# Softmax factors of a forgetting-attention layer: the 12-element steps move from GpSimd to VectorE

## The chip, the cores and the metric

The kernel runs on one core of one Trainium2 chip. The metric is the device time of one execution in microseconds (us). TensorE is called PE below (its weight loads PEld), VectorE DVE, ScalarE ACT, GpSimd POOL and the queue of transfers SP.

## The reference

One decoder layer over 1040 tokens (16 learned ones in front of 1024 real ones), width 1024, all in float32. A normalised input is projected to q, k, v, a forget gate, an output gate z and four inputs of a gated convolution. Attention has 8 heads of 64:

```
s = einsum('bqhd,bkhd->bhqk', q, k) * scale + c[t] - c[s]      # c: running sum of log forget gates
s = where(key_pos <= t, s, -inf)
p = softmax(s, axis=-1);  out = einsum('bhqk,bkhd->bqhd', p, v)
```

The attention output and the convolution output are RMS-normalised by groups of 64 columns, multiplied by SiLU gates, concatenated, sent through one output projection, added to the residual and normalised.

## The kernel before

Every float32 product is made of three matmuls over a high part and a low part of each operand. The program has three stretches. Up to some 178 us it projects q, k, v and the gate. From 178 to 480 us it sweeps the 8 heads. Then comes the output projection.

The middle stretch is what the change touches. For each head the queries are taken in two halves, `c = 0` (query blocks 0 to 3) and `c = 1` (blocks 4 to 7), so there are 16 half-heads. The half with `c = 1` of a head comes first. For one half:

- `s_step` (lines 605 to 614): for a block of 128 queries j and a chunk i of its keys (`SCH[j]`, one to three chunks), two matmuls make the scores in a PSUM bank `pn`, DVE takes their negated row maximum into `nmx[c]` (L609 for the last chunk, which is masked, L612 for the others), ACT writes exp(score - chunk maximum) into the SBUF tile `pn[j]` and the sum of each row into `smx[c]` (L613).
- `s_end` (lines 616 to 636) comes once per half, so 16 times. It turns the 4 x 3 chunk maxima and sums of a row into a factor per chunk: row maximum `mx` (L619, DVE), difference `e` (L621, POOL), its exp (L622, ACT), `e` times the sums `t` (L624, POOL), their sum over three chunks `s` (L626 and L627, two additions on POOL), reciprocal (L628, DVE), factor `fc` (L630, POOL). Then POOL multiplies each chunk of `pn[j]` by its factor (L635: 9 pieces for `c = 1`, 5 for `c = 0`).
- `t_step` (L645 to L657): PE transposes a 128-key column of `pn[j]` for the blocks of the half into a PSUM bank `pt` (two buffers); at the diagonal DVE clears and transposes a 32-column corner (L649, L651); ACT writes the high part `ph` (L654), DVE the low part `pl` (L115, the helper `lo_vec`).
- `v_step` (L669): two matmuls of `ph` and `pl` with v into the bank `po`; `fold` (L680, L681) brings the two halves of `po` together.

Between these steps PE is given projection work of the other branch as filler: `block_steps` (L165, tile `pj`), three matmuls at a time, with its followers on DVE and ACT (the gate's SiLU at L433 to L438, the convolution at L451 to L467, group norms at L404 to L417). The weights of the next block are split into `wmhi` (L112, POOL) and `wmlo` (L115, DVE). The first convolution product `cv` is POOL's (L460), the next two and the scaling are DVE's (L461 to L463).

The order of PE's matmuls in this stretch is written out: `weave` mixes steps by given durations, and `pinned` keeps that order. `s_end` stands at a given place in it (`S_AT`, `WAIT`). The other engines' instructions are ordered by the framework's planner, from its own estimate of when each one's inputs are ready; each engine then works through its queue in that order. SP issues the loads of the next head's q, k, v and of weights; `s_end` issues no transfer.

Of the kernel before, what the change touches and what calls it, by code (L numbers as in the profile page):

```python
# [12 lines left out]
ALU = mybir.AluOpType  # L13
AX = mybir.AxisListType
# [3 lines left out]
P = 128  # L18
# [17 lines left out]
def hybrid_kernel(ctx, tc, hT, h, w_q, w_vf, w_m, w_o, gn, bf, cw, ga, gc, gf, out):  # L36
    nc = tc.nc
# [531 lines left out]
    nmx, smx = [], []  # L569
# [46 lines left out]
    def s_end(c):  # L616

        mx = pnp.tile([P, 4], F32, name="mx")
        nc.vector.tensor_reduce(mx, nmx[c], AX.X, ALU.min)  # L619
        e = pnp.tile([P, 4, 3], F32, name="e")  # L620
        nc.gpsimd.tensor_tensor(e, mx.unsqueeze(2).broadcast_to([P, 4, 3]), nmx[c], ALU.subtract)  # L621
        nc.scalar.activation(e, e, AF.Exp)  # L622
        t = pnp.tile([P, 4, 3], F32, name="t")
        nc.gpsimd.tensor_mul(t, e, smx[c])  # L624
        s = pnp.tile([P, 4], F32, name="s")
        nc.gpsimd.tensor_add(s, t[:, :, 0], t[:, :, 1])  # L626
        nc.gpsimd.tensor_add(s, s, t[:, :, 2])  # L627
        nc.vector.reciprocal(s, s)  # L628
        fc = pnp.tile([P, 4, 3], F32, name="fc", bufs=2)
        nc.gpsimd.tensor_mul(fc, e, s.unsqueeze(2).broadcast_to([P, 4, 3]))  # L630
        for i in range(3):
            for j in range(4 * c, 4 * c + 4):
                if i < len(SCH[j]):
                    k0, w = SCH[j][i]
                    nc.gpsimd.tensor_scalar(pn[j][:, k0:k0 + w], pn[j][:, k0:k0 + w], fc[:, j % 4, i:i + 1], 1.0,  # L635
                                            ALU.mult, ALU.mult)
# [79 lines left out]
    for g in range(-1, 2 * HEADS):  # L716
        steps = []
        if g >= 0 and g % 2 == 0 and g // 2 + 1 < HEADS:
            steps.append((0.0, 0.0, lambda hd=g // 2 + 1: load_head(hd)))
        if g + 1 < 2 * HEADS:  # L720
            hd, c = (g + 1) // 2, g % 2
            todo = [(2 * SCH[j][i][1] / 2400.0, lambda hd=hd, j=j, i=i: s_step(hd, j, i))
                    for j in range(4 * c, 4 * c + 4) for i in range(len(SCH[j]))]
            lo, hi = S_AT[g % 2 if g >= 0 else 2]
            spread(steps, todo, lo, hi)
            steps.append((hi, WAIT[g % 2 if g >= 0 else 2], lambda c=c: s_end(c)))
        if g >= 0:
            hd, c = g // 2, 1 - g % 2
            box = {}
            tv = []  # L730
            nk = 4 * c + 5
            for kt in range(nk + V_LAG):
                if kt < nk:
                    w = 512 - max(0, (kt - 4 * c) * P - 32)
                    tv.append((w / 1200.0, lambda c=c, kt=kt, box=box: t_step(c, kt, box)))
                if kt >= V_LAG:
                    w = 512 - max(0, (kt - V_LAG - 4 * c) * P - 32)
                    tv.append((w / 1200.0, lambda hd=hd, c=c, kt=kt - V_LAG, box=box: v_step(hd, c, kt, box)))
            spread(steps, tv, T_AT[c], V_END)
            steps.append((0.99, 0.0, lambda hd=hd, c=c, box=box: fold(hd, c, box)))  # L740
            if g > 0 and (g - 1) % 4 >= 2:
                steps.append((0.05, SOON, lambda m=(g - 1) // 4, c=g % 2: finish_soon(m, c)))
        stages.append([(x, s) for _, x, s in sorted(steps, key=lambda t: t[0])])
# [164 lines left out]
```

## Time and profile before

| | |
|---|---|
| median of 3 runs | 595.57 us (594.65 to 597.58) |
| profiled execution, its own time | 596.83 us |
| its span, first to last instruction | 595.1 us |
| PE busy in the span | 578.0 us (97%) |
| DVE busy | 377.9 us (64%) |
| ACT busy | 285.4 us (48%) |
| POOL busy | 168.0 us (28%) |
| mean granted TensorE clock | 0.995 |

A busy PE is not a PE at its peak: matmuls are pipelined and their ends are modelled. What PE really loses is seen in the distances between the starts of its instructions. A row of the timeline gives start, duration, engine, line, operation, output and inputs with their sizes, and behind it the idle time before it with what ended it.

### The profile page before, as it was taken

The page shows a single profiled execution, that of the slowest core. Times are in us where ns is not written, and L with a number is a line of the kernel's source. Part 1 is how long each engine was busy: PE and PEld are TensorE (multiplying, and loading weights), DVE is VectorE, ACT ScalarE, POOL GpSimd, SP SyncE. Part 2 cuts the span into 40 slices and gives each one's busy share as a digit, 9 for nine tenths or more (in the row PEclk, how much of TensorE's full clock was granted, in tenths as well). Part 3 has the DMA queues.
Part 4 walks back from the last instruction along what each step waited for, and adds up shares of the span by engine and source line. Part 5 has one row for each costly group of instructions (what it writes and reads, how often), then busy time and mean ns, then how long its engine had stood idle before and what let it go on. Part 6 is the DMA issues. An engine that isn't in the chain of part 4 may idle for free.

```text
span 595.1 us, 9156 instructions
## 1 busy us (share of the span) xinstructions
PE 578.0 (97%) x3230; PEld 509.6 (86%) x3230; DVE 377.9 (64%) x834; ACT 285.4 (48%) x667; POOL 168.0 (28%) x290
## 2 busy tenths in 40 slices
PE   9999999999998999999999999999999999899995
PEld 6888999999997889988879997889998887688884
DVE  5415851133367686879776888868869777947432
ACT  5355431131044575556764655747636676705221
POOL 1002010121027244151243254430552416710000
PEclk9999999999999999999999999999999999899999
DMA  8764594249811605415126134251350227453201
GB/s 287 237 194 141 195 341 142 70 147 280 262 39 36 144 35 135 120 57 155 44 75 143 71 108 112 75 143 37 111 197 16 73 88 243 171 205 113 100 35 70
DMA packets 35221, 78.14 MB, mean 131 GB/s; under 512 B 4024, under 2 KB 13384, under 8 KB 35176
## 3 DMA queue, kind: packets, MB, share of 16 engines
q1 hardware_dynamic: 35032, 77.57, 41.6%
q8 instruction: 25, 0.41, 0.3%
q14 instruction: 20, 0.16, 0.1%
q10 hardware_dynamic: 144, 0.00, 0.0%
HBM read 55.92 MB, written 21.64 MB: 130 GB/s over the span
## 4 chain that ended last, share of the span: by engine, by line
PE 71%; DMA 10%; DVE 6%; POOL 4%; ACT 3%; issue 3%; SPq 2%; POOLq 0%; ACTq 0%; DVEq 0%
PE pj L165 30%; PE ps L324 8%; PE p L788 8%; PE pt L645 5%; PE po L669 5%; PE pj L788 4%; PE ps L165 4%; DMA k<-kd 3%; DMA ht<-in_h 3%; PE pn L605 3%; PE pn L606 3%; DMA xs<-in_hT 2%; DVE mlo L115 2%; POOL pn L635 1%; DMA wm<-in_w_m 1%
## 5 line engine op out<-in xcount | busy, mean ns | idle before, releaser
L165 PE MATMUL pj<-xhi,wmhi 128*128 128x512 f32 (+1 forms) x384 | 144.9, 377 | 1.0 <-DVE kf L275 0.5
L165 PE MATMUL pj<-xhi,wmlo 128*128 128x512 f32 (+1 forms) x384 | 137.1, 357 | 0.0
L165 PE MATMUL pj<-xlo,wmhi 128*128 128x512 f32 (+1 forms) x384 | 136.8, 356 | 0.0
L613 ACT ACTIVATE pn<-pn,nmx 128x328 f32<-128x328 f32 (+6 forms) x112 | 60.5, 541 | 52.7 <-DVE nmx L612 27.9
L165 PEld LDWEIGHTS pj<-xhi,wmlo 128*128 128x128 f32 x384 | 72.2, 188 | 8.4
L165 PEld LDWEIGHTS pj<-xhi,wmhi 128*128 128x128 f32 x384 | 72.6, 189 | 6.2 <-issue 1.4
L165 PEld LDWEIGHTS pj<-xlo,wmhi 128*128 128x128 f32 x384 | 72.8, 190 | 3.8
L654 ACT CAST ph<-pt 128x512 fp32r<-128x512 f32 (+4 forms) x112 | 49.6, 445 | 51.0 <-PE po L669 23.3
L635 POOL TENSOR_SCALAR pn<-pn,fc 128x328 f32<-128x328 f32 (+4 forms) x112 | 69.3, 639 | 1.6
L115 DVE TENSOR_TENSOR pl<-pt,ph 128x512 fp32r<-128x512 f32 (+1 forms) x96 | 54.6, 572 | 20.2 <-ACT ph L654 19.5
L112 POOL TENSOR_SCALAR wmhi<-wm 128x1024 fp32r<-128x1024 f32 x24 | 26.2, 1093 | 141.2 <-DMA wm<-in_w_m 81.8
L645 PE MATMUL pt<-ident,pn 128*128 128x128 f32 x288 | 47.4, 273 | 3.9 <-POOL pn L635 2.2
L645 PEld LDWEIGHTS pt<-ident,pn 128*128 128x128 f32 x288 | 36.3, 140 | 14.4 <-POOL pn L635 3.6
L115 DVE TENSOR_TENSOR wmlo<-wm,wmhi 128x1024 fp32r<-128x1024 f32 x24 | 29.4, 1223 | 18.0 <-POOL wmhi L112 17.9
L609 DVE CUSTOM_DVE_ANT_0 pn<-pn,maskn 128x328 f32<-128x328 f32 (+3 forms) x64 | 31.9, 500 | 11.0 <-PE pn L606 9.3
L669 PE MATMUL po<-ph,v 128*128 128x512 f32 (+4 forms) x112 | 37.0, 336 | 0.0
L605 PE MATMUL pn<-k,q 128*128 128x328 f32 (+6 forms) x112 | 36.6, 328 | 0.1
L606 PE MATMUL pn<-k,q 66*128 66x328 f32 (+6 forms) x112 | 36.1, 322 | 0.0
L669 PE MATMUL po<-pl,v 128*128 128x512 f32 (+1 forms) x96 | 33.2, 350 | 0.0
L788 PE MATMUL p<-whi,mlo 128*128 128x512 f32 (+1 forms) x77 | 30.2, 392 | 2.4 <-DVE mlo L115 2.4
L165 PE MATMUL ps<-xhi,wmhi 128*128 128x346 f32 (+1 forms) x96 | 31.0, 323 | 1.1 <-ACT qraw L240 1.1
L612 DVE TENSOR_REDUCE nmx<-pn 128x1 f32<-128x346 f32 (+4 forms) x48 | 24.8, 521 | 9.6 <-PE pn L606 9.6
(227 smaller groups left out, 1229.5 us busy)
## 6 DMA issues: line engine op xcount, KB each, us to landing
wm<-in_w_m SPq DMA_DIRECT2D x24, 512.0 KB, 3.8
k<-kd SPq DMA_DIRECT2D x24, 260.0 KB, 5.3
q<-qd SPq DMA_DIRECT2D x24, 256.0 KB, 5.9
vd<-vv SPq DMA_DIRECT2D x9, 512.0 KB, 2.9
v<-vd SPq DMA_DIRECT2D x8, 576.0 KB, 6.5
ht<-in_h SPq DMA_DIRECT2D x8, 512.0 KB, 5.6
yd<-gy SPq DMA_DIRECT2D x16, 256.0 KB, 2.8
q<-in_w_o SPq DMA_DIRECT2D x8, 512.0 KB, 4.5
```

What stands on the lines that cost most here:

```text
L115: nc.vector.tensor_tensor(lo, src, f(hi), ALU.subtract)
L165: ins = nc.tensor.matmul(ps[:, :w], wt[:, k, :], xt[:, t0:t0 + w], start=(k == 0 and n == 0), stop=(k == KT - 1 and n == 2))
L324: nc.tensor.matmul(ps[c][:P if n == P else 48, :260], x[k][:, ts_] if n == P else x[:, k, :], w[k][:, 260 * c:260 * c + 260], start=(k == ...
L605: pinned(nc.tensor.matmul(ps[:, :w], q1[:, qs], k1[:, ks], start=True, stop=False))
L606: pinned(nc.tensor.matmul(ps[:, :w], q2[:DH + 2, qs], k2[:DH + 2, ks], start=False, stop=True))
L609: nc.vector.tensor_tensor_reduce(ps[:, :w], ps[:, :w], maskn[:, MASKW - w:], op0=ALU.add, op1=ALU.min, scale=-1.0, scalar=-NEG, accum_out= ...
L613: nc.scalar.activation(pn[j][:, ks], ps[:, :w], AF.Exp, bias=nmx[c][at], scale=-1.0 if last else 1.0, accum_out=smx[c][at])
L635: nc.gpsimd.tensor_scalar(pn[j][:, k0:k0 + w], pn[j][:, k0:k0 + w], fc[:, j % 4, i:i + 1], 1.0, ALU.mult, ALU.mult)
L645: pinned(nc.tensor.transpose(pt[:, q0:q0 + P], pn[j][:, ks], ident))
L654: nc.scalar.copy(ph[:, at:], pt[:, at:])
L669: pinned(nc.tensor.matmul(po[:, at:], v2[:, vk, :], t[:, at:], start=(kt == 0 and i == 0), stop=(kt == 4 * c + 4 and i == len(parts) - 1)))
L788: ins = nc.tensor.matmul(held[n][:, :w], a[:, tt], b[:, cs], start=(e == ORDER[0] and i == 0), stop=(e == ORDER[-1] and i == 2))
```

## The change

In `s_end` the four instructions on `e`, `t` and `fc` are issued on VectorE, and the two additions over the three chunks become one `tensor_reduce` there. The exp stays on ScalarE, the scaling of `pn` (L635) on GpSimd.

```
         mx = pnp.tile([P, 4], F32, name="mx")
         nc.vector.tensor_reduce(mx, nmx[c], AX.X, ALU.min)
         e = pnp.tile([P, 4, 3], F32, name="e")
-        nc.gpsimd.tensor_tensor(e, mx.unsqueeze(2).broadcast_to([P, 4, 3]), nmx[c], ALU.subtract)
+        nc.vector.tensor_tensor(e, mx.unsqueeze(2).broadcast_to([P, 4, 3]), nmx[c], ALU.subtract)
         nc.scalar.activation(e, e, AF.Exp)
         t = pnp.tile([P, 4, 3], F32, name="t")
-        nc.gpsimd.tensor_mul(t, e, smx[c])
+        nc.vector.tensor_mul(t, e, smx[c])
         s = pnp.tile([P, 4], F32, name="s")
-        nc.gpsimd.tensor_add(s, t[:, :, 0], t[:, :, 1])
-        nc.gpsimd.tensor_add(s, s, t[:, :, 2])
+        nc.vector.tensor_reduce(s, t, AX.X, ALU.add)
         nc.vector.reciprocal(s, s)
         fc = pnp.tile([P, 4, 3], F32, name="fc", bufs=2)
-        nc.gpsimd.tensor_mul(fc, e, s.unsqueeze(2).broadcast_to([P, 4, 3]))
+        nc.vector.tensor_mul(fc, e, s.unsqueeze(2).broadcast_to([P, 4, 3]))
```

(Three of the instructions, on `e`, `t` and `fc`, have two inputs in SBUF; the reduce has one.)

## Rows read from the trace of the kernel before

**Rows 1.** The page's chain that ended last: shares of the span by engine.
```profile
PE 71%; DMA 10%; DVE 6%; POOL 4%; ACT 3%; issue 3%; SPq 2%; POOLq 0%; ACTq 0%; DVEq 0%
```

**Rows 2.** Busy us (and instructions) by engine in the stretch of the heads.
```profile
178.00:480.00 302.00, 297.82 (x1663) 261.77 (x1662) 233.66 (x570) 177.44 (x451) 119.62 (x218) 1.00 0.33 97
```

**Rows 3.** Waits of PE and PEld, 178:480: who <- whom, us, times, longest.
```profile
PEld pt L645 <- POOL pn L635: 3.6, 4, 1.7
...
PE pt L645 <- POOL pn L635: 2.2, 2, 1.5
```

**Rows 4.** Instructions by line: xcount, ns min/median/max, first and last start us.
```profile
L621 POOL TENSOR_TENSOR e<-mx,nmx x16: 206/209/1239, 178.9 to 473.3; 128x12 f32<-128x12 f32 x16
...
L622 ACT ACTIVATE e<-e x16: 202/215/223, 179.2 to 474.0; 128x12 f32<-128x12 f32 x16
```

**Rows 5.** Timeline of DVE, 129:132, a chain of dependent additions.
```profile
131.03 0.76 DVE L362 TENSOR_TENSOR acc<-acc,lf 128x8 f32<-128x8 f32 x4
```

**Rows 6.** Timeline of POOL, 176:184.5, the first set of small steps.
```profile
178.95 0.21 POOL L621 TENSOR_TENSOR e<-mx,nmx 128x12 f32<-128x12 f32 x1
179.48 0.89 POOL L624 TENSOR_TENSOR t<-e,smx 128x12 f32<-128x12 f32 x1 [0.32 <-ACT e L622]
...
182.25 1.10 POOL L630 TENSOR_TENSOR fc<-e,s 128x12 f32<-128x12 f32 x1 [0.29 <-DVE s L628]
183.45 1.11 POOL L635 TENSOR_SCALAR pn<-pn,fc 128x328 f32<-128x328 f32 x2
```

**Rows 7.** Timeline of PE, 183:186.5, behind the first set.
```profile
183.97 0.28 PE L606 MATMUL pn<-k,q 66*128 66x272 f32 x1
185.76 0.66 PE L645 MATMUL pt<-ident,pn 128*128 128x128 f32 x4 [1.51 <-POOL pn L635]
```

**Rows 8.** Timeline of DVE, 296:301, the seventh set.
```profile
298.55 1.27 DVE L115 TENSOR_TENSOR wmlo<-wm,wmhi 128x1024 fp32r<-128x1024 f32 x1
299.78 0.19 DVE L628 RECIPROCAL s<-s 128x4 f32<-128x4 f32 x1
```

**Rows 9.** Timeline of PE, 301:304.5, behind the seventh set.
```profile
302.32 0.40 PE L165 MATMUL pj<-xlo,wmhi 128*128 128x512 f32 x1
302.55 0.39 PE L165 MATMUL pj<-xhi,wmlo 128*128 128x512 f32 x1
303.64 0.66 PE L645 MATMUL pt<-ident,pn 128*128 128x128 f32 x4 [0.70 <-POOL pn L635]
```

**Rows 10.** Timeline of PE, 382:383.5, behind the eleventh set.
```profile
382.77 0.40 PE L165 MATMUL pj<-xhi,wmlo 128*128 128x512 f32 x1
383.26 0.44 PE L645 MATMUL pt<-ident,pn 128*128 128x128 f32 x2
```

**Rows 11.** Timeline of DVE, 355.5:361, the tenth set.
```profile
355.52 0.69 DVE L115 TENSOR_TENSOR pl<-pt,ph 128x512 fp32r<-128x512 f32 x1
...
356.26 1.28 DVE L461 SCALAR_TENSOR_TENSOR cv<-cx,cwt,cv 128x1024 f32<-128x1024 f32 x1
...
359.77 0.18 DVE L628 RECIPROCAL s<-s 128x4 f32<-128x4 f32 x1 [0.66 <-POOL s L627]
359.91 0.62 DVE L115 TENSOR_TENSOR pl<-pt,ph 128x416 fp32r<-128x416 f32 x1
```

**Rows 12.** Timeline of POOL, 356:361.5, the tenth set.
```profile
356.37 1.24 POOL L621 TENSOR_TENSOR e<-mx,nmx 128x12 f32<-128x12 f32 x1
```

**Rows 13.** Timeline of PE, 359:361, during the tenth set.
```profile
359.64 0.39 PE L165 MATMUL pj<-xhi,wmlo 128*128 128x512 f32 x1
360.67 0.30 PE L645 MATMUL pt<-ident,pn 128*128 128x128 f32 x1 [0.64 <-DVE pl L115]
```

**Rows 14.** Timeline of PE, 355:364, the transposes that reuse the bank of 355.52.
```profile
357.81 0.38 PE L645 MATMUL pt<-ident,pn 128*128 128x128 f32 x2
```

**Rows 15.** Timeline of DVE, 455:460, the fifteenth set.
```profile
456.11 0.59 DVE L115 TENSOR_TENSOR pl<-pt,ph 128x416 fp32r<-128x416 f32 x1 [0.34 <-ACT ph L654]
```

**Rows 16.** Timeline of PE, 454:457.5, the transposes that reuse that bank.
```profile
456.85 0.30 PE L645 MATMUL pt<-ident,pn 128*128 128x128 f32 x1
```

## The prediction

> **What bounds the kernel now.** I read the page's chain first. PE holds 71% of it, POOL 4%, DVE 6% [rows 1]: the small steps can only be worth what PE waits for them, not what they last. The busy times of the stretch from 178 to 480 us say the same: of 302 us PE is busy 297.82, DVE 233.66 (77%), POOL 119.62 (40%) [rows 2]. Next the waits of PE and its weight loads in this stretch, for everything that ends with the scaled scores `pn`: four waits of the weight loads, 3.6 us, and two of matmuls, 2.2 us [rows 3]. The matmul's wait is the same stall as the weight load's, seen a second time, so there are four stalls in sixteen calls of `s_end`. Twelve calls hand over early enough that PE never waits for POOL.
>
> What each stall costs is read from PE's starts. Three-matmul groups of 512 columns go at 302.55 - 302.32 = 0.23 us each [rows 9]. A start later than that is lost time:
> - first set: 185.76 - 183.97, less 0.12 for 272 columns: 1.67 us [rows 7];
> - seventh set: 303.64 - 302.55 - 0.23 = 0.86 us [rows 9];
> - eleventh set: 383.26 - 382.77 - 0.23 = 0.26 us [rows 10];
> - the fifteenth repeats the pattern at 461.9 us with about 0.2 us.
>
> Together 2.99 us. One more stall hangs on the small steps by a detour. At 360.67 PE stands 360.67 - 359.64 - 0.23 = 0.80 us, not for `pn` but for a PSUM bank that DVE's `pl` still reads [rows 13]; this `pl` started at 359.91, behind a reciprocal that had DVE idle for 0.66 us until POOL's sum came [rows 11]. With it all that the change can win on the way of the factors is 3.8 us, 0.64% of the time.
>
> **The change part by part.**
>
> Removed from POOL: five instructions in each of 16 sets, some 0.21 us each where nothing disturbs them (the median of the difference) and up to 1.24 us where something does [rows 4], so 16 x 5 x 0.21 = 17 us of an engine that is 40% busy [rows 2]. By itself this is worth nothing; what counts is the time to the factor. Also gone are the crossings between POOL and DVE around the reciprocal.
>
> Added to DVE: four instructions a set. The nearest row is a chain of dependent additions of 128x8 on DVE: four in 0.76 us, 0.19 us each with the gap between them [rows 5]. The new shapes have 12 elements, so I take 0.19 us, with 0.16 (no gap) and 0.25 as bounds. That is 16 x 4 x 0.19 = 12.2 us, and takes DVE in this stretch from 233.66 to 245.8 us, 81%.
>
> The new time to the factor, from the start of `e` to the first `pn` piece: `e` 0.19; the two crossings to ACT and back together 179.48 - 179.16 - 0.215 = 0.10 (between POOL and ACT [rows 4, 6]; I take the same for DVE); the exp 0.215 [rows 4]; `t`, the sum, the reciprocal and `fc` 4 x 0.19 = 0.76; to POOL 183.45 - 183.35 = 0.10 [rows 6]. That is 1.37 us if nothing stands between. In the first set this piece took 183.45 - 178.95 = 4.50 us [rows 6].
>
> What the four stalls give back:
> - Seventh set: the reciprocal stood on DVE behind the split of a weight block, 1.27 us from 298.55, and started at 299.78 [rows 8]. With all steps on DVE in one run this one long instruction can still stand in front of one of them, but the sum no longer crosses engines ahead of it. I count all 0.86 us. Bounds 0 and 0.86.
> - Eleventh and fifteenth: 0.26 + 0.2 = 0.46 us, all of it, since a quarter of a microsecond is less than the steps get shorter. Bounds 0 and 0.46.
> - First set: here the POOL steps were stretched to 0.89 and 1.10 us [rows 6] in the time in which DVE worked on the convolution. The same shows in the tenth set: `e` took 1.24 us instead of 0.21 and ended at 357.61, just behind DVE's L461 at 357.54 [rows 11, 12]. POOL waits while DVE works on such an operand pair. The convolution's three instructions (L461 and its two followers) are still to be done, and the `pn` pieces, which start earlier now, meet them in place of the small steps. I take half of 1.67, 0.83 us. Bounds 0 and 1.67.
> - Tenth set: the wait of 0.66 us on DVE goes, but 4 x 0.19 = 0.76 us of new instructions come in front of the same `pl`. I take 0. Bounds -0.3 (if two of the steps follow a wait for the exp) and +0.80.
>
> Sum: 0.86 + 0.46 + 0.83 = 2.15 us won.
>
> [...]
>
> What it costs: DVE works in order, so each set puts 0.76 us of new work, and a wait for the exp of up to 0.10 + 0.215 = 0.32 us, in front of whatever is queued there: the `pl` of the running transposes, the followers of the projection blocks, then the next scores' maxima. Who waits is PE, for the bank that `pl` frees two transposes later. The spare time differs: the `pl` of 355.52 ended at 356.21, and the transposes that reuse its bank started at 357.81, 1.60 us later [rows 11, 14]; the one of 456.11 ended at 456.70 with 0.15 us to spare [rows 15, 16]. A delay of 0.76 + 0.32 = 1.08 us is hidden under 1.6 and not under 0.15, where 0.93 us would be lost. Near the sixteen sets I find the small spare time in two, the sixth (0.4 us) and the fifteenth; elsewhere it is 1.5 us or more. In the fifteenth DVE was idle for 0.34 us just before [rows 15], which takes up `e`. I count 0.9 us for both together. Bounds 0 and 1.9.
>
> Sum: -2.15 + 0.9 = -1.25 us. The profiled execution took 596.83 us (span 595.1 and 1.7 around it), so 595.6 by its own time; it lies 1.26 us over the median of 595.57, and against that median the forecast is 594.3 us, -0.2%. A measurement of this kernel tells about 0.5%, or 3 us, from no change, so this is no change that can be seen.
>
> **The rivals.**
> - *All stalls go.* The new 1.37 us hold everywhere, the pieces of the first set don't meet the convolution, DVE's work is hidden: -3.8 us, 591.8. For it: in each of these places the factors come late by a wait that the change takes away [rows 3, 6, 8, 11]. Against: rows 11 and 12, and that it needs all five places at once, with no cost.
> - *DVE waits in line for ACT.* A step that needs the exp stands directly behind `e`, and ACT has other work in front of the exp. Place: DVE's queue, in each set; price: delay less spare time. With 0.76 + 0.32 and half a microsecond of other work on ACT (one cast of `ph` or one exp of scores) the delay is 1.6 us: it equals the usual spare time [rows 11, 14], and from there on it decides. At 2.1 us, one instruction more, each of fourteen sets loses 0.5 and the two tight ones 1.9: 14 x 0.5 + 2 x 1.9 = 10.8; where this holds for every other set, 5.4, less the 2.15 won: +3.3 us, 598.8. For it: DVE is at 77% and goes to 81%, and 0.66 us of such idling are in the trace already [rows 11]. Against: the planner puts ready work between; at 298.55 it put 1.27 us of it in front of the reciprocal [rows 8].
> - *The lock moves on.* By that mechanism (rows 11 and 12) the first set gives nothing and the others as above: -0.4 us, 595.1.
> - *The order changes elsewhere.* Only PE's order is written out; the planner lays the other queues anew. A weight split or a convolution step that lands in front of a `pl` costs up to its 1.27 us [rows 8] less the spare time. It can go either way; I let it widen the range by 2 us on both sides.
>
> **How the numbers follow.** Forecast with the moved lock, between -3 and +3 us: 0.56. All stalls go, or nearly all with a lucky new order, beyond -3 us: 0.20. DVE's waiting or an unlucky order, beyond +3 us: 0.24. The range reaches from 591.4, a little below the case in which every stall goes, to 599.4, a little above the slower rival.
>
> **What would show it.** In the trace after: `e` to `pn` under 2.2 us in most sets; the four waits of the weight loads for POOL's `pn` down from 3.6 us to under 1.5, the first set's the largest left; POOL's `pn` pieces of the first set with durations over 1 us beside L461 to L463; DVE some 246 us busy in the stretch; new waits of PE for `pl` of about 1 us in all. The forecast is wrong if PE's waits for DVE grow past 4 us, or if those for `pn` vanish and none comes in their place.

## The result: 1.2% slower, and the profile after

The changed kernel took 602.43 us (median of six runs, 599.34 to 604.63) against 595.11 us for the kernel before beside it (593.98 to 597.58): a ratio of 1.0117, 95% interval 1.0080 to 1.0155. The forecast was 594.3 us with a range up to 599.4, so it was wrong, and on the wrong side. The profiled execution took 604.03 us with a span of 602.3 us, that of before 596.83 and 595.1: the two traces differ by about the same 7.2 us as the medians. From the reciprocal on, line numbers are one lower in the changed kernel (the factor is L629, `pn` is scaled in L634, transposed from L644 and multiplied with v in L668).

Busy times by engine (PE, PEld, DVE, ACT, POOL), then granted clock, DMA share and GB/s, of the same stretch, which now lasts to 488 us [rows 2]:

```profile
178.00:488.00 310.00, 302.80 (x1667) 265.04 (x1666) 242.41 (x635) 178.73 (x453) 99.24 (x138) 0.99 0.33 94
```

DVE has 8.8 us more work (12.2 were forecast; some of the added time overlaps its neighbours, as at 180.60 us below, where a step of 0.16 us is followed after 0.12) and POOL is relieved. PE has more to wait for: 7.2 us are not busy where there were 4.2, and some of its busy time runs at a lower clock (0.99 granted over the stretch, 1.00 before). The waits of PE and its weight loads in that stretch (who <- whom, us, times, longest) [rows 3]:

```profile
PEld pt L644 <- POOL pn L634: 6.4, 5, 2.4
PEld po L668 <- DVE ph L115: 1.6, 2, 0.9
PEld po L668 <- DVE pl L115: 1.0, 1, 1.0
```

The waits for `pn` that were to shrink from 3.6 us to under 1.5 grew to 6.4, and 2.6 us for `ph` and `pl` stand beside them. The steps themselves are as short as forecast in the median; three of the 48 with two inputs took longer, 0.28 to 0.58 us (count, ns min/median/max, first and last start) [rows 4]:

```profile
L624 DVE TENSOR_TENSOR t<-e,smx x16: 157/164/583, 181.9 to 481.7; 128x12 f32<-128x12 f32 x16
L626 DVE TENSOR_REDUCE s<-t x16: 148/166/197, 183.2 to 481.9; 128x4 f32<-128x12 f32 x16
L629 DVE TENSOR_TENSOR fc<-e,s x16: 158/172/395, 184.1 to 482.6; 128x12 f32<-128x12 f32 x16
```

So the steps are short, but the chain is long. From the start of the maximum (L619) to the end of the factor the mean over sixteen sets is 3.33 us before and 3.86 us after. The first set shows why; DVE's timeline (start, us, instruction):

```profile
178.37 0.16 DVE L619 TENSOR_REDUCE mx<-nmx 128x4 f32<-128x12 f32 x1
...
179.40 1.28 DVE L461 SCALAR_TENSOR_TENSOR cv<-cx,cwt,cv 128x1024 f32<-128x1024 f32 x1 [0.86 <-POOL cv L460]
180.60 0.16 DVE L621 TENSOR_TENSOR e<-mx,nmx 128x12 f32<-128x12 f32 x1
180.72 1.28 DVE L462 SCALAR_TENSOR_TENSOR cv<-cx,cwt,cv 128x1024 f32<-128x1024 f32 x1
181.92 0.16 DVE L624 TENSOR_TENSOR t<-e,smx 128x12 f32<-128x12 f32 x1
182.04 1.23 DVE L463 TENSOR_TENSOR cv<-cv,rbc 128x1024 f32<-128x1024 f32 x1
183.18 0.16 DVE L626 TENSOR_REDUCE s<-t 128x4 f32<-128x12 f32 x1
183.26 0.68 DVE L472 TENSOR_TENSOR zc<-pj,rbc 128x512 f32<-128x512 f32 x1
183.85 0.17 DVE L627 RECIPROCAL s<-s 128x4 f32<-128x4 f32 x1
...
184.15 0.17 DVE L629 TENSOR_TENSOR fc<-e,s 128x12 f32<-128x12 f32 x1
```

In front of every step that follows the maximum other work stands in DVE's queue, most of it long. Before, POOL's queue held only the steps in thirteen of the sixteen sets (in the sixth, seventh and eighth a weight split of 1.05 us stood among them), and only the maximum and the reciprocal passed through DVE's [rows 6, 8]. A late factor is not yet lost time: the tenth set's takes longest, 7.12 us instead of 4.10, and PE does not wait for it. What PE makes of it in the first set [rows 7], from PE's timeline:

```profile
184.35 0.28 PE L606 MATMUL pn<-k,q 66*128 66x272 f32 x1
...
186.80 0.66 PE L644 MATMUL pt<-ident,pn 128*128 128x128 f32 x4 [2.16 <-POOL pn L634]
```

The stretch behind it, busy by engine, with the granted clock as the third column from the end:

```profile
188.00:191.00 3.00, 3.00 (x11) 2.41 (x10) 2.08 (x3) 1.00 (x2) 2.37 (x4) 0.50 0.00 0
```

The stall is 186.80 - 184.35 - 0.12 = 2.33 us instead of 1.67. Then the granted clock fell to 0.50 (before, behind the stall of 1.67 us, it was 1.00 from 188 to 191 us), and PE's 512-column matmuls started 189.95 - 189.52 = 0.43 us apart instead of 0.23 (PE's timeline):

```profile
189.52 0.63 PE L165 MATMUL pj<-xlo,wmhi 128*128 128x512 f32 x1
189.95 0.63 PE L165 MATMUL pj<-xhi,wmlo 128*128 128x512 f32 x1
```

PE executes the same 3230 matmuls in the same order in both kernels, so each one's start can be compared. Of 7.38 us in all: the start-up +0.4; the first set +2.2 (0.65 stall, 1.6 clock); 267 us, before the sixth set, -0.9; the sixth +1.4; the seventh +0.6; the ninth +0.5; the tenth -0.4; 450 us +0.3; the fifteenth +3.4, of which 1.4 is clock (0.50 from 468 to 471 us); the rest -0.1. The -0.9 at 267 us is there in e4, e6 and e11 below as well, of which two leave the steps on POOL, so it does not come from the steps. Nor does it come from another order: DVE and POOL have the same instructions in the same order there in both traces. In the trace of before DVE's `gsl`, with two inputs in SBUF, lasts through a `pn` piece (264.75 to 265.31 us) and a weight split of POOL (265.27 to 266.32); in the trace after it starts 0.09 us ahead of that piece, which now takes 1.03 us instead of 0.56, and ahead of the split at 268.48 (DVE's timeline, before and after):

```profile
264.74 2.15 DVE L115 TENSOR_TENSOR gsl<-gy,gsh 128x512 fp32r<-128x512 f32 x1 [1.16 <-ACT gsh L407]
```

```profile
267.39 0.69 DVE L115 TENSOR_TENSOR gsl<-gy,gsh 128x512 fp32r<-128x512 f32 x1 [1.21 <-ACT gsh L407]
```

In the sixth set PE waits for `pl`. What was in front of it, from POOL's timeline, then DVE's, then PE's (in brackets the idle time before and its releaser):

```profile
281.76 1.05 POOL L112 TENSOR_SCALAR wmhi<-wm 128x1024 fp32r<-128x1024 f32 x1 [4.33 <-PE pj L165]
```

```profile
282.24 0.58 DVE L624 TENSOR_TENSOR t<-e,smx 128x12 f32<-128x12 f32 x1
```

```profile
287.00 0.34 PE L668 MATMUL po<-pl,v 128*128 128x160 f32 x1 [0.81 <-DVE pl L115]
```

`t` ran 0.58 us instead of 0.16 and ended at 282.82, just behind POOL's split of a weight block, at 282.81. The fifteenth set shows the same with `fc`, and both of PE's waits (POOL's, DVE's, PE's timeline):

```profile
463.38 1.20 POOL L112 TENSOR_SCALAR wmhi<-wm 128x1024 fp32r<-128x1024 f32 x1 [14.41 <-PE pj L165]
```

```profile
464.20 0.40 DVE L629 TENSOR_TENSOR fc<-e,s 128x12 f32<-128x12 f32 x1
```

```profile
465.48 0.28 PE L668 MATMUL po<-ph,v 128*128 128x32 f32 x1 [0.80 <-DVE ph L115]
...
468.04 0.69 PE L644 MATMUL pt<-ident,pn 128*128 128x128 f32 x2 [1.00 <-POOL pn L634]
```

The factor is 1.5 us later there than before, shifts ahead of it taken out. The `pn` pieces then take 0.5 us more up to the transposes, because one of them lasts 1.61 us instead of 0.64 beside DVE's split (before, only the first was longer, 1.04 us instead of 0.54). These are POOL's timeline and DVE's:

```profile
465.85 1.61 POOL L634 TENSOR_SCALAR pn<-pn,fc 128x456 f32<-128x456 f32 x1
```

```profile
465.45 1.49 DVE L115 TENSOR_TENSOR wmlo<-wm,wmhi 128x1024 fp32r<-128x1024 f32 x1
```

Late factor and longer pieces together are the 2.0 us without the clock; the wait for `ph` lies in front of the wait for `pn` and adds nothing to it.

The chain of the page after adds up to 41% of the span (PE 29%): following back breaks off on the way, so it can't be set against [rows 1].

### The profile page after: what moved, and what is told of

Same layout as the page of the kernel before. It is cut to its first block, busy times and chain, and to the rows that moved or that the text cites. A ratio compares the mean times of both kernels' runs of the same rounds, so it can differ in the third digit from the quotient of the medians.

```text
span 602.3 us, 9231 instructions
## 1 busy us (share of the span) xinstructions
PE 582.5 (97%) x3230; PEld 512.5 (85%) x3230; DVE 385.9 (64%) x898; ACT 286.4 (48%) x667; POOL 146.4 (24%) x210
## 5 line engine op out<-in xcount | busy, mean ns | idle before, releaser
L634 POOL TENSOR_SCALAR pn<-pn,fc 128x328 f32<-128x328 f32 (+4 forms) x112 | 70.7, 651 | 104.7 <-DVE fc L629 77.7
L644 PE MATMUL pt<-ident,pn 128*128 128x128 f32 x288 | 48.4, 278 | 5.0 <-POOL pn L634 4.7
L644 PEld LDWEIGHTS pt<-ident,pn 128*128 128x128 f32 x288 | 36.8, 142 | 15.9 <-POOL pn L634 6.4
L668 PE MATMUL po<-ph,v 128*128 128x512 f32 (+4 forms) x112 | 37.3, 337 | 1.0 <-DVE ph L115 1.0
L668 PE MATMUL po<-pl,v 128*128 128x512 f32 (+1 forms) x96 | 33.4, 351 | 0.8 <-DVE pl L115 0.8
```

Source lines behind the costliest of these rows:

```text
L644: pinned(nc.tensor.transpose(pt[:, q0:q0 + P], pn[j][:, ks], ident))
L668: pinned(nc.tensor.matmul(po[:, at:], v2[:, vk, :], t[:, at:], start=(kt == 0 and i == 0), stop=(kt == 4 * c + 4 and i == len(parts) - 1)))
```

## The experiments

Ratios are to the kernel before beside them, with 95% intervals; a set is one call of `s_end`, counted from 1.

**1. Make the factors earlier: less on DVE between the steps (e1_close).** Theory A is that what the planner puts between the steps makes the factors late and that this costs the time. With less there, the mean from maximum to factor falls to about 2.3 us, the stalls of the seventh and fifteenth set go, the first set's falls to about 1.4, and the time to about 595 us, 593.5 to 597. DVE work named later in the program is ordered behind `fc`; work named earlier (the convolution in the first set, a `pl` in most) can still stand between.

```diff
...
-        nc.vector.tensor_mul(fc, e, ...)
+        last = nc.vector.tensor_mul(fc, e, ...)
+        if behind_fc:
+            behind_fc.pop().__exit__(None, None, None)
+        behind_fc.append(tc.issue_after(last.ins))
+        behind_fc[0].__enter__()
...
```

> The changed kernel with the same instructions, but VectorE work that the program names after the small steps is queued behind the factor of each set, so that it can't go between the steps. [...] Theory B (the extra work on VectorE and its waits for ScalarE in VectorE's queue cost the time): the same instructions are there and VectorE now idles for the exp, so 602 or more.

Measured: 606.94 us, 1.0197 (1.0173 to 1.0220), slower still. The mean from maximum to factor did fall, to 2.84 us. The first set's stall was 1.80 us (2.33 in the changed kernel, 1.67 before), the seventh set's stall for `pn` was gone, and so was most of the waiting for `pn`, 2.2 us against 6.4:

```profile
PEld pt L648 <- POOL pn L638: 2.2, 2, 1.9
```

So the late factors do come from what stands between the steps. But the sixth set alone lost 6.1 us against before, clock included (512-column matmuls behind its stall started 284.40 - 283.83 = 0.57 us apart, behind the same transposes in e9 280.94 - 280.62 = 0.32). The timelines of DVE, POOL and PE there:

```profile
279.38 1.03 DVE L629 TENSOR_TENSOR fc<-e,s 128x12 f32<-128x12 f32 x1
...
281.49 1.59 DVE L115 TENSOR_TENSOR wmlo<-wm,wmhi 128x1024 fp32r<-128x1024 f32 x1
283.00 0.94 DVE L115 TENSOR_TENSOR pl<-pt,ph 128x416 fp32r<-128x416 f32 x2
```

```profile
279.35 1.05 POOL L112 TENSOR_SCALAR wmhi<-wm 128x1024 fp32r<-128x1024 f32 x1 [4.27 <-PE pj L165]
```

```profile
283.73 0.45 PE L648 MATMUL pt<-ident,pn 128*128 128x128 f32 x1 [3.61 <-DVE pl L115]
```

`fc` took 1.03 us, as long as POOL's split beside it, and the work held back behind the factor (the second half of the split, then `pl`) left PE standing for 3.61 us. Late factors are thus not the whole matter: what protects them starves `pl`. The theory that the time comes back with them fell.

**2. Half of the sets (e3_even_dve).** The steps on DVE for `c == 1` (the odd sets) only.

```diff
+        v = nc.vector if c == 1 else nc.gpsimd
...
-        nc.vector.tensor_tensor(e, ...)
+        v.tensor_tensor(e, ...)
...
```

> The small steps on VectorE for the halves with query blocks 4 to 7 only (sets 1, 3, 5, ... counted from 1), on GpSimd as before for the others. Theory A: the sets whose factor PE waits for are all of this half, so most of the loss stays: 599 to 602 us, with the stall behind the first set, the clock fall behind it and the stall behind set 15. Theory B: half of the added work, half of the loss: 598.5, without any one place that holds most of it.

Measured: 600.71 us, 1.0104 (1.0074 to 1.0134). In its trace the first set lost 2.3 us (its clock fell again, to a mean of 0.63 from 186.6 to 191 us), the seventh 0.6, the ninth 0.5, the fifteenth 2.0, and the sixth, now on POOL, 0.2 to 0.3. The losses sit in single sets, and a set put back on POOL has next to none.

**3. The work without the chain (e4_load, e6_load_one).** The kernel before, with four added DVE steps in each set whose result nobody reads: subtractions of two SBUF inputs (e4), or one-input reductions (e6).

```diff
+        d = pnp.tile([P, 4, 3], F32, name="d")
+        for n in range(4):
+            nc.vector.tensor_tensor(d, mx..., nmx[c], ALU.subtract)
```

```diff
+        d = pnp.tile([P, 4], F32, name="d")
+        for n in range(4):
+            nc.vector.tensor_reduce(d, nmx[c], AX.X, ALU.min)
```

> The kernel before, small steps on GpSimd, and in each set four more 128x12 subtractions on VectorE that nobody reads, each behind the one before it. It doubles the suspected cost on VectorE without its place in the chain of the factors. Theory A: within 1 us of the kernel before, 594.5 to 596.5. Theory B: 600 to 602, as the changed kernel.

> The kernel before with four more small VectorE instructions in each set that nobody reads, as in the run with subtractions, but each a reduction with one input in SBUF instead of a subtraction with two. In that run the subtraction of set 6 at 278.30 us took 1010 ns while GpSimd split a weight block (1052 ns), and the stall behind it cost 2.9 us of PE. Theory D (a GpSimd instruction holds a VectorE instruction with two SBUF inputs, and with it the whole queue): no small instruction over 0.3 us, set 6 without its stall, 594.5 to 595.5. Theory B (the work): 597 as with the subtractions.

Measured: 597.09 us, 1.0030 (1.0014 to 1.0047), and 595.65 us, 1.0016 (1.0003 to 1.0030). Both lie just above what theories A and D said. With two inputs there is one place with a large loss, the sixth set, 3.1 us, of which 1.6 is clock (0.99 granted from 178 to 488 us, 1.00 in e6); with one input the same place loses 0.7. That step on DVE's timeline in e4, POOL's instruction beside it, the same place in e6 (DVE, POOL), and the durations of all 64 added steps (count, ns min/median/max) in e4 and in e6:

```profile
278.30 1.01 DVE L624 TENSOR_TENSOR d<-mx,nmx 128x12 f32<-128x12 f32 x1
```

```profile
278.25 1.05 POOL L112 TENSOR_SCALAR wmhi<-wm 128x1024 fp32r<-128x1024 f32 x1
```

```profile
278.77 0.15 DVE L624 TENSOR_REDUCE d<-nmx 128x4 f32<-128x12 f32 x1
```

```profile
278.72 1.04 POOL L112 TENSOR_SCALAR wmhi<-wm 128x1024 fp32r<-128x1024 f32 x1
```

```profile
L624 DVE TENSOR_TENSOR d<-mx,nmx x64: 153/171/1010, 178.9 to 476.4; 128x12 f32<-128x12 f32 x64
```

```profile
L624 DVE TENSOR_REDUCE d<-nmx x64: 133/165/196, 177.4 to 474.0; 128x4 f32<-128x12 f32 x64
```

A 0.17 us step with two inputs took 1.01 us and ended at 279.31, just behind POOL's 1.05 us split, at 279.30; of 64 with one input none took over 0.20 us, and the one beside the split took 0.15. Beside another POOL instruction a step was not held: in the changed kernel the `e` at 236.51 us took 0.17 us in the middle of POOL's 0.95 us memset (L584, from 235.85), which reads nothing. The four added steps cost 0.2% (one input) to 0.3% (two) of the 1.2%, and most of it in one set.

**4. Move the convolution out of the first set (e5_close_conv).** As experiment 1, and the four convolution steps are named one block later.

```diff
-                nc.gpsimd.tensor_scalar(cv, cx[:, 2:1026], ...)
...
+                def conv():
+                    nc.gpsimd.tensor_scalar(cv, cx[:, 2:1026], ...)
...
+                box["conv"] = conv
...
         if c == 0:
...
+                box.pop("conv")()
```

> As the run in which later work is queued behind the factor, and the four convolution steps (one on GpSimd, three on VectorE) are named by the program one block of projections later, so that they too come behind the factor in sets 1 and 10. Theory A: the first set's factor comes under 2.5 us after its maximum, its stall of PE goes altogether, and the time is some 1.5 us under the run without this: 592 to 594.5, under the kernel before. Theory B: 602 or more.

Measured: 605.50 us, 1.0162 (1.0135 to 1.0189). From maximum to factor the first set took 2.07 us, but its stall was only 0.39 us shorter than before (1.28 us); the sixth set lost 6.2 us as in experiment 1. Timelines of DVE and POOL:

```profile
178.37 0.17 DVE L633 TENSOR_TENSOR fc<-e,s 128x12 f32<-128x12 f32 x1
178.46 1.28 DVE L463 SCALAR_TENSOR_TENSOR cv<-cx,cwt,cv 128x1024 f32<-128x1024 f32 x1
```

```profile
178.71 5.08 POOL L642 TENSOR_SCALAR pn<-pn,fc 128x328 f32<-128x328 f32 x4 [1.26 <-DVE fc L633]
```

Four `pn` pieces took 5.08 us beside the convolution; before, four took 2.26. Most of what the factor won, the pieces lost: this is the rival "The lock moves on" (POOL held while DVE works, [rows 11, 12]), shown in this run.

**5. Which sets hold the loss (e8_thirteen, e9_three, e11_first).** On DVE in all sets but 1, 6 and 15; in these three alone (if they hold the loss, theory C: 600 to 602 us); in the first alone.

```diff
+        calls.append(c)
+        v = nc.vector if len(calls) not in (1, 6, 15) else nc.gpsimd
...
```

> The small steps on VectorE in thirteen sets, and on GpSimd as before in sets 1, 6 and 15 alone. Theory C (the loss sits in these three places, where VectorE's queue makes the factors or the low parts of the running transposes late, and in the slow clock behind them; comparing the two traces they hold 2.0 + 1.3 + 3.3 of 7.4 us): 595 to 596.5 us. Theory B (the added work on VectorE costs in each set): thirteen sixteenths of the loss stay, 601.

> The other half of the run with thirteen sets: the small steps on VectorE in sets 1, 6 and 15 alone, on GpSimd in the rest. [...] If what happens there needs the added work in the sets before them too: under 598.

> The small steps on VectorE in set 1 alone. Theory C: its stall grows from 1.67 to 2.3 us and the clock falls behind it, 0.65 + 1.4 = 2.0 us in the trace: 596 to 597. If the planner's order elsewhere gives or takes more than this one place: outside 595 to 598.

Measured: e8 595.37 us, 1.0023 (1.0003 to 1.0042); e9 600.05 us, 1.0086 (1.0054 to 1.0118); e11 595.89 us, 1.0012 (0.9989 to 1.0036). Thirteen sets make 0.2%, three make 0.9%, together 1.1 of the 1.2. In e9's trace the three lost 0.65, 1.3 and 3.5 us. The time of e11 alone cannot be told from the kernel before.

The first set gives a warning. Its stall is the same in e9 and in e11; the clock behind it is not (PE's timeline, then the busy times of 186.6 to 190 with the clock third from the end; e9 first, then e11):

```profile
184.19 0.28 PE L606 MATMUL pn<-k,q 66*128 66x272 f32 x1
186.65 0.55 PE L650 MATMUL pt<-ident,pn 128*128 128x128 f32 x3 [2.17 <-POOL pn L640]
```

```profile
186.60:190.00 3.40, 3.35 (x19) 2.92 (x20) 2.54 (x4) 1.69 (x3) 3.40 (x5) 1.00 0.00 0
```

```profile
184.18 0.28 PE L606 MATMUL pn<-k,q 66*128 66x272 f32 x1
186.63 0.69 PE L650 MATMUL pt<-ident,pn 128*128 128x128 f32 x2 [2.16 <-POOL pn L640]
```

```profile
186.60:190.00 3.40, 3.37 (x12) 2.94 (x13) 1.93 (x3) 1.29 (x3) 3.40 (x5) 0.52 0.00 0
```

2.34 and 2.33 us of standing still: once the clock stays at 1.00, once it falls to 0.52. In e11's profiled execution the set cost 2.1 us, 1.5 more than in e9's. So a stall of 2.3 us was followed by the fall in one execution and not in another, and one profile can't say how often. The mean clocks of all runs say something of it: of the six runs of the changed kernel three had 0.987 to 0.988 and took 602.0 to 604.6 us, as the profiled one did, and three had 0.994 to 0.995 and took 599.3 to 602.8 us.

**6. Keep the clock up (e7_warm).** The changed kernel, with eight matmuls of 512 columns, whose result is overwritten, in the first and the fifteenth set's stall. The theory: the clock falls because PE stands there. Then it stays up, the factors come no earlier, and the time is about 600.5 us; if the clock falls for another reason, 602.5 to 603.5 us and a granted clock still halved at these places.

```diff
...
+        if kt == 0 and c == 1 and box["hd"] in (0, 7):
+            for n in range(8):
+                pinned(nc.tensor.matmul(pt, xhi[n][:, :P], xhi[n][:, :512], start=True, stop=True))
...
```

> The changed kernel with eight 512-column matmuls into the transposes' bank (which the transposes overwrite) in front of the first transposes of sets 1 and 15, so that PE works in the 2.3 us and the 1.2 us in which it stood there. [...]

Measured: 600.79 us, 1.0095 (1.0074 to 1.0117), 1.6 us under the changed kernel's median. The work in the stall, from PE's timeline, and the stretch behind it:

```profile
183.47 2.04 PE L644 MATMUL pt<-xhi 128*128 128x512 f32 x8
```

```profile
188.00:191.00 3.00, 3.00 (x17) 2.51 (x16) 1.65 (x4) 1.15 (x4) 1.40 (x3) 1.00 0.00 0
```

The same stretch had 0.50 in the changed kernel; from 468 to 471 us it was 1.00 here and 0.50 there. The clock's share is then 0.2% of the 1.2% or a little more, since the eight matmuls outlast the fifteenth set's stall (2.7 us lost there instead of 2.0). As the intervals of 1.0095 and 1.0117 overlap, that is a size, not a proof.

**7. Other cuts (p_lnexp, e10_eleven).** In p_lnexp the kernel before keeps its steps on POOL, and the reciprocal, its only DVE step, goes to ACT:

```diff
-        nc.vector.reciprocal(s, s)
+        nc.scalar.activation(s, s, AF.Ln)
+        nc.scalar.activation(s, s, AF.Exp, scale=-1.0)
```

> The kernel before with the reciprocal taken off VectorE: exp(-ln(s)) in two ScalarE instructions, the other small steps on GpSimd as before. The factors no longer pass through VectorE's queue, in which the reciprocal stood behind long work for 1.0 to 1.3 us in sets 6, 7, 8 and 11. If that queue is what makes them late, the stalls behind sets 7 and 11 (0.86 and 0.26 us) go: 593.5 to 594.7, under the kernel before. If ScalarE's queue holds them as long: 595 to 597.

Measured: 601.15 us, 1.0104 (1.0085 to 1.0123), against an expected gain. POOL's timeline in the fifteenth set (2.84 us lost):

```profile
460.01 1.46 POOL L112 TENSOR_SCALAR wmhi<-wm 128x1024 fp32r<-128x1024 f32 x1 [0.72 <-PE pj L165]
461.43 0.21 POOL L631 TENSOR_TENSOR fc<-e,s 128x12 f32<-128x12 f32 x1
```

The same pattern on another queue: 1.46 us of ready work slid in front of the last step. Here a removed crossing did not help, since the planner could put long work into the gap.

e10 takes from e8 the two further sets that lost in its trace (7 and 9) back to POOL: `not in (1, 6, 7, 9, 15)`.

> A version that may beat both: VectorE in the eleven sets in which no run showed PE waiting longer for it, GpSimd in sets 1, 6, 7, 9 and 15. Compared with the run of thirteen sets the stalls of sets 7 and 9 (0.63 and 0.52 us more than before) go back, those won at 267.6 and 360.7 us of the trace (0.94 and 0.77) stay: 593 to 594.5, some 0.2% under the kernel before. If the planner's new order costs as much elsewhere: 594.5 to 596.

Measured: 593.89 us, 0.9990 (0.9966 to 1.0015). Its waits of the weight loads for `pn`:

```profile
PEld pt L650 <- POOL pn L640: 2.8, 4, 1.7
```

3.6 us before, 2.8 here, 6.4 in the changed kernel. In time it can't be told from the kernel before, so no version here is shown to be faster than that.

## Why the prediction was wrong, step by step

**What bounds the kernel** held: PE's order and its few waits decide, and the loss appeared as longer and new waits of PE.

**The prices of the steps** held: 0.16 to 0.17 us for an instruction where I took 0.19. The same number of steps that nobody reads cost 0.2% (e6).

**The step that failed is "That is 1.37 us if nothing stands between"** and the stalls that were counted as won on it. On DVE something stands between in every set: 5.95 us instead of 5.35 from maximum to factor in the first set, 5.11 instead of 4.08 in the seventh, 5.14 instead of 3.81 in the fifteenth. I had the evidence in [rows 8] and even used it, against the rival of DVE waiting in line for ACT ("the planner puts ready work between"); but I let "one" long instruction stand there, where a chain of six dependent steps gives the planner a gap behind each. With fewer of these gaps filled the waits for `pn` fell to 2.2 us and the seventh set's stall went, as forecast (e1). Term by term:
- seventh set, 0.86 counted as won: its `pn` stall grew to 1.31 us, and 0.6 was lost;
- eleventh, 0.26 won: it stands at 0.26 us as before; fifteenth, 0.2 won: 2.0 lost, and 1.4 by the clock;
- first set, 0.83 won (0 by "The lock moves on"): 0.65 lost, and 1.6 by the clock;
- tenth set, 0 counted: 0.4 won, though its factor came latest of all;
- ninth set, not named: 0.5 lost.

**The cost of the late `pl`** was the right mechanism in the right sets, with too small a size: 0.9 us counted for the sixth and fifteenth together, 1.4 us measured in the sixth alone. In the fifteenth PE waited 1.03 us for `ph`, the same kind of delay, but in front of a wait for `pn` that would have held it as long. What lacked was the hold in the other direction: I had read POOL waiting while DVE works [rows 11, 12] and put no price on DVE waiting while POOL works. The runs show it: steps of 0.17 us took 1.03 us (e1) and 1.01 us (e4) beside a split of 1.05. The trace of before had it too, unread: the `gsl` of 264.74 us, 2.15 us beside POOL's work instead of 0.69.

**The clock** stood in no term and no rival: 2.9 us of the profiled 7.4.

**The rivals.** "The lock moves on" was right in e5. In the changed kernel it shows in the fifteenth set (the piece of 1.61 us), but not where it was placed, in the first, where the factor itself came later than the convolution. "DVE waits in line for ACT" ends near the measured side with another mechanism: DVE was not idle for ACT, it was filled. "The order changes elsewhere" was the right idea at a wrong place: not elsewhere, but within the steps. And "wrong if PE's waits for DVE grow past 4 us" named the wrong wait, since 2.6 us went to DVE and 6.4 to `pn`.

Left open: why equal stalls are followed by a lower clock in one execution and not in another, and whether `gsl` is held in every execution of the kernel before; in the two traces that makes 0.9 us.

## What to carry to other kernels

Don't price a chain of small dependent steps by the sum of their durations: on an engine that takes its queue in order and has ready work, as DVE does here (idle for 0.66 us until POOL's sum came, its `pl` behind that [rows 11]), count one long instruction behind each step that has to wait, compare the delay with the time until PE needs the result, and prefer a queue that holds little else, even if its instructions are slower (0.21 us on POOL against 0.17 on DVE here). Before moving work between DVE and POOL, look at what long instruction of the other runs at that time (a step of 0.17 us took up to 1.03 us beside POOL's split, four POOL pieces 5.08 us instead of 2.26 beside DVE's convolution), and give a longer stall of PE a price in clock too (1.4 to 1.6 us where the clock fell).

## What the runs showed of the hardware

- A DVE step of 128x12 with two inputs took 1.03 us (e1) and 1.01 us (e4) instead of 0.17 beside GpSimd's weight split of 1.05 us, ended with the split, and the next instruction in DVE's queue started behind it (280.42 us in e1, 279.35 in e4). Beside a GpSimd memset of 0.95 us, which reads nothing, such a step took its 0.17 us (after). Of 64 one-input steps of that size none took over 0.196 us, the one beside a split 0.15 (e6).
- DVE's `gsl` of 128x512, beside the same instructions of GpSimd, took 0.69 us after, where it came first, and 2.15 us before, where it lasted through a `pn` piece and the split. After, the `pn` piece that started 0.09 us behind it took 1.03 us instead of 0.56.
- In the stretch behind a 2.3 us stall of PE the granted clock was 0.50 to 0.52 in some executions (188 to 191 us after, 186.6 to 190 us in e11) and 1.00 in another (e9). Where it fell it cost 1.4 to 1.6 us. With eight matmuls in the stall it was 1.00 in the profiled execution (e7).
